# The sums of gated products for the down-projection, moved into the up-projection

## The chip, the cores and the metric

The kernel runs on one core of a Trainium2 chip. A core has a matrix engine (TensorE, PE in the profile, with PEld for its weight loads), VectorE (DVE), ScalarE (ACT) and GpSimd (POOL), each with its own instruction queue, and SyncE (SP), which here only issues DMA transfers. POOL issues transfers too. Instructions of one queue run in order; between queues, semaphores hold an instruction until what it needs is there. The metric is the device time of one execution in microseconds (us); lower is better. Before the change it is 1100.41 us, the median of three runs (1100.34, 1100.41 and 1101.11).

## The reference

A trunk of two layers over a residual of 512 tokens x 1024 features in float32. Each layer has attention (dilated sliding windows in layer 0, forgetting attention in layer 1) and then a gated feed-forward with a causal convolution, which is where the change lies:

```python
D_MODEL, SEQ, D_FF, CONV_W = 1024, 512, 2816, 3

def conv_ffn(xn, w_up, cw, cb, w_down):
    a = xn @ w_up                                    # 512 x 1024 times 1024 x 5632
    T = a.shape[1]
    ap = jnp.pad(a, ((0, 0), (CONV_W - 1, 0), (0, 0)))
    a = sum(ap[:, j:j + T] * cw[j] for j in range(CONV_W)) + cb
    gate, val = jnp.split(a, 2, axis=-1)
    return (jax.nn.gelu(gate, approximate=True) * val) @ w_down
```

## The kernel before

**Products in three parts.** A float32 operand is split into a high part, a rounded copy, and a low part, the rest. A product is then three matmuls (L289, L290 and L291, in `mm3`). A high part is a copy on ACT (`Pair.high`, L713). A low part is a subtraction on DVE (`Pair.low`, L720), or for some tiles a negated copy on ACT (L715) and an accumulating transfer that POOL issues (L716).

**The up-projection** (`ffn`). The 2816 gate columns and as many value columns are cut into 22 chunks of 128. A chunk of gate or value is a PSUM bank of 128 columns x 512 tokens. Chunks 0 and 1 come from a step ahead of the loop and chunks 20 and 21 are made plainly behind it. The 18 between are made as 9 pairs of chunks (`Pair`), in a loop over `pairs`. A pair's product is cut into 2 x 2 blocks (gate and value, halves of the inputs, halves of the tokens LO and HI) and made with seven block products p_1 to p_7 instead of eight. For that it needs sums of weight blocks (S1, S2, S3, S4; L697, on DVE), copies of partial results out of PSUM (`keep`, L736, on ACT, to tiles `csum`) and sums of results (`sum_3` L773, `sum_4` L778, `sum_1` L783, on DVE). `p_2` writes to banks that `sum_4` reads.

**Taps, gate and product.** In the iteration that makes pair i, the two chunks of pair i-1 are finished: `tap` for gate and value (ACT scales into `bb` at L635, DVE adds two shifted columns at L636 and L637), GELU on ACT (L655), and the product of both on DVE (L662) to a tile `hc` of 128 x 512. The even chunk of a pair is called a in the loop, the odd one b. When the next chunk's product is made, POOL first stores the previous `hc` to the DRAM tile hD (L660).

**The down-projection** (`down`) goes over 11 pairs j of chunks 2j and 2j+1, with the same scheme of seven products. `pair_load` reads the even chunk and the second token half of the odd one from hD into a tile `dact` (L804, L805). `pair_sums` forms three sums of 128 x 256 in it on DVE (L811 to L813), and POOL stores the last of them to the DRAM tile sD (L814). `pair_highs` and `pair_lows` split the four blocks (ACT L821, DVE L825). Later, `load_two` reads sD and the odd chunk again (L831, L832) and `pair_two` forms the remaining operands. The first pair's sums are made at the end of the up-projection's loop, those of pairs 1 to 3 during chunks 20 and 21, and the others three pairs ahead of their products.

**What sets the order.** It is written by hand: each queue has its instructions in the order in which the Python code issues them, as in this stretch of the loop's iteration (n is the next pair, p this one):

```python
            p.sum_4()
            if n and prev:
                n.high("S3")
            if prev:
                b.gelu()
            ...
            if prev:
                p.p_2()
            if n:
                n.s2()
            if prev:
                b.product()
            if n:
                n.take("A12")
                n.s4()
                n.keep_1()
```

`n.low("S3")` and `n.low("S2")` come behind it, and `prev.sum_1()`, `a.tap(0)` at the start of the next iteration. Tiles come from pools of fixed size that are reused in turn (`t8` 16 slots, `t4` 10, `t2` 8; `hc`, `csum` and the down stage's sums are from `t2`); a tile's first writer waits until the slot's last user is done. Weights arrive through `W`, which loads some blocks ahead.

Of the kernel before, what the change touches and what calls it, by code (L numbers as in the profile page):

```python
# [9 lines left out]
F32 = mybir.dt.float32  # L10
# [3 lines left out]
ALU = mybir.AluOpType  # L14

D = 1024
T = 512
# [4 lines left out]
NF = DFF // 128  # L22
# [6 lines left out]
ND = NF // 2  # L29
# [86 lines left out]
def trunk_kernel(ctx, tc, x, norm_gains, w_qkv_a, w_o_a, w_q_b, w_o_b, kv_norm, w_kvf, b_f,  # L116
                 w_up, conv_w, conv_b, w_down, rope, out):
    nc = tc.nc
    act, dve, pool, pe, sp = nc.scalar, nc.vector, nc.gpsimd, nc.tensor, nc.sync
# [8 lines left out]
    def t8(shape, dt=F32, name="t8"):  # L128
        return p8.tile(shape, dt, tag="t8", name=name)

    def t4(shape, dt=F32, name="t4"):
        return p4.tile(shape, dt, tag="t4", name=name)

    def t2(shape, dt=F32, name="t2"):
        return p2.tile(shape, dt, tag="t2", name=name)
# [490 lines left out]


    def ffn(l, bd, cp, nxt, gain, ahead):
        hD = tc.dram_tile([NF, 128, T], F32, name="hD")
        sD = tc.dram_tile([ND, 128, 256], F32, name="sD")  # L630
        hc = {}

        def tap(bb, c, s, ps):
            ch = c + s * NF
# [4 lines left out]
        class Chunk:  # L639
# [15 lines left out]
                act.activation(self.bb[:, 0, :], self.bb[:, 0, :], AF.Gelu_apprx_tanh)  # L655

            def product(self):
                c = self.c
                if c - 1 in hc:
                    pool.dma_start(hD[c - 1], hc.pop(c - 1))  # L660
                hc[c] = t2([128, T], name="hc")
                dve.tensor_tensor(hc[c], self.bb[:, 0, :], self.bb[:, 1, :], ALU.mult)  # L662
                del self.bb

        xT = None
        XA, XB = [], []
# [19 lines left out]
        class Pair:  # L686
# [52 lines left out]
            def p_1(self):  # L739
                self.G = self.new_banks()  # L740
                self.prod("A11", self.at(self.G, HI), X(0), LO, True)
# [53 lines left out]

        acts, one, two, raws, later2 = {}, {}, {}, {}, {}
        H = slice(0, 512), slice(512, 1024)
        a11, s1_, s3_, s2_ = (slice(i * 256, i * 256 + 256) for i in range(4))

        def pair_load(j):  # L800

            if j < ND:
                acts[j] = k = t8([128, 1024], name="dact")
                sp.dma_start(k[:, 0:512], hD[2 * j])  # L804
                sp.dma_start(k[:, s2_], hD[2 * j + 1, :, 256:512])  # L805

        def pair_sums(j):

            pair_load(j + 1)
            k = acts[j]  # L810
            dve.tensor_tensor(k[:, s3_], k[:, a11], k[:, s1_], ALU.subtract)  # L811
            dve.tensor_tensor(k[:, s1_], k[:, s1_], k[:, s2_], ALU.add)
            dve.tensor_tensor(k[:, s2_], k[:, s1_], k[:, a11], ALU.subtract)  # L813
            pool.dma_start(sD[j], k[:, s2_])  # L814

        def pair_highs(j):

            raws[j] = [*W.take(2), acts.pop(j)]
            one[j] = [t8([128, 2, 1024], F32R, name="w") for _ in range(3)]
            for w, r in zip(one[j], raws[j]):  # L820
                act.copy(w[:, 0], r)  # L821

        def pair_lows(j):
            for w, r in zip(one[j], raws.pop(j)):
                dve.tensor_tensor(w[:, 1], r, w[:, 0].bitcast(F32), ALU.subtract)  # L825

        def load_two(j):

            if j < ND:
                later2[j] = k, r4 = t4([128, 768], name="dact2"), t2([128, 512], name="dt4")  # L830
                sp.dma_start(k[:, 0:256], sD[j])  # L831
                sp.dma_start(k[:, 256:768], hD[2 * j + 1])  # L832
                sp.dma_start(r4, dT[l][j, :, 1536:2048])

        def pair_two(j):

            if j >= ND:
                return
            r1, = W.take(1)
            load_two(j + 1)  # L840
            k, r4 = later2.pop(j)
            w, ac = t8([128, 2, 1024], F32R, name="w"), t8([128, 2048], F32R, name="w")
            t4l = t2([128, 512], F32R, name="dt4l")
            act.copy(w[:, 0], r1)
            dve.tensor_tensor(k[:, 0:256], k[:, 256:512], k[:, 0:256], ALU.subtract)
            act.copy(ac[:, 1536:2048], r4)
            act.copy(ac[:, 0:768], k)
            dve.tensor_tensor(w[:, 1], r1, w[:, 0].bitcast(F32), ALU.subtract)
            dve.tensor_tensor(t4l, r4, ac[:, 1536:2048].bitcast(F32), ALU.subtract)
            dve.tensor_tensor(ac[:, 768:1536], k, ac[:, 0:768].bitcast(F32), ALU.subtract)  # L850
            av = ac[:, 0:1536].rearrange("p (s c) -> p s c", s=2)
            two[j] = (av[:, 0], av[:, 1]), (w[:, 0], w[:, 1]), (ac[:, 1536:2048], t4l)
# [30 lines left out]
        def p_21(j, bp):  # L883
            product_of(db[bp + 2, 0], two[j][0], 2, two[j][2], H[0], bp)

        def p_12(j, bp):
            product_of(db[bp, 1], two[j][0], 0, two[j][1], H[1], bp)
# [9 lines left out]
        def down(nxt, ahead):  # L897
            pair_highs(3)
            for bp in range(2):
                for j in range(2):  # L900
                    mul_one(j, bp)
            for j in range(1, ND - 2):
                if j > 1:
                    mul_one(j, 0)
                    mul_one(j, 1)
                if j + 3 < ND:
                    pair_sums(j + 3)
                    pair_lows(j + 2)
                    pair_highs(j + 3)
                elif j + 3 == ND:  # L910
                    pair_lows(j + 2)
                    load_two(0)
            pair_two(0)
            pair_two(1)
            for bp in range(2):
                for j in (ND - 2, ND - 1):
                    mul_one(j, bp)
                combine_one(bp)
                pair_two(bp + 2)
            one.clear()  # L920
            for bp in range(2):
                for j in range(2):
                    p_21(j, bp)
                    p_1(j, bp)
            pair_two(4)

            last = range(ND - LAST, ND)
            for j in range(2, ND - 2):
                for bp in range(2):
                    p_21(j, bp)  # L930
                if 2 <= j - 2 < ND - LAST - 2:
                    p_1(j - 2, 0)
                    p_1(j - 2, 1)
                    two.pop(j - 2)
                pair_two(j + 3)
            W.n_get += 3 * ND
            for i, b in enumerate(nxt.order):
                if ahead and i < 3:
                    W.split(W.n_split + 1)
                if b >= 2:  # L940
                    nxt.half(i, 0, 1, db[b, 1])
                    for j in range(ND - 2, ND):
                        p_21(j, b - 2)
                    nxt.half(i, 1, 0, db[b, 0])
                    for bp in range(2):
                        p_1(last[0] - 2 + i, bp)
                    if ahead and i == 1:
                        W.split(W.n_split + 1)
                    continue
                narrow = nxt.narrow and i == NB - 1  # L950
                for j in last:
                    p_11(j, b, slice(0, 256) if narrow else slice(0, 512))
                if narrow:
                    nxt.part(b, 0, db[b, 0][:, 0:256], 0)
                else:
                    nxt.half(i, 0, 0, db[b, 0])
                for j in last:
                    p_12(j, b)
                if not narrow:
                    nxt.half(i, 1, 1, db[b, 1])  # L960
                    continue
                nxt.part(b, 1, db[b, 1], 512)
                for j in last:
                    p_11(j, b, slice(256, 512))
                nxt.part(b, 2, db[b, 0][:, 256:512], 256)
# [135 lines left out]
        W.ahead_dma = 2  # L1101
        W.high_added()
        nxt.mix.gain = load_gain(gain, f"gain{l}3")
        pair_sums(0)
        a, b = m
        banks = [begun[1], bank([128, T], name="up")]
        up(*begun, range(4, KD))
# [7 lines left out]
        b.tap(1)  # L1115
        b.gelu()
        pair_highs(0)
        pair_sums(1)
        last = Chunk(NF - 2, banks)
        banks = prev.new_banks()  # L1120
        up(W.get(), banks[0], range(KD))
# [3 lines left out]
        last.tap(1)  # L1125
        last.gelu()
        pair_highs(1)
        pair_sums(2)
        up(W.get(), banks[1], range(KD))
        last.product()  # L1130
        last = Chunk(NF - 1, banks)
# [2 lines left out]
        last.tap(1)  # L1134
        last.gelu()
        pair_highs(2)
        pair_sums(3)
        pair_lows(2)
        last.product()
        pool.dma_start(hD[NF - 1], hc.pop(NF - 1))  # L1140

        down(nxt, ahead)
        W.ahead = 4
# [679 lines left out]
    for n in range(N + 3):  # L1823
        live = n < N
        if live:
            j, i = units[n]
# [93 lines left out]
```

## Time and profile before

| | |
|---|---|
| median of three runs | 1100.41 us |
| the profiled execution | 1101.14 us, of it 1099.4 us span; granted clock 0.999 |
| busy in the span | PE 1090.0 us (99%), DVE 903.0 (82%), ACT 752.7 (68%), POOL 216.5 (20%) |
| DMA | 255.22 MB, mean 232 GB/s |
| `hc` stores (L660) | 44 of 256 KB, median 7.6 us to landing |
| sD stores (L814) | 22 of 128 KB, median 5.5 us to landing |
| `dact` loads from hD | 44 of 256 KB (5.8 us), 22 of 128 KB (5.0 us) |
| the pair loop | `p_2` starts between 240.05 and 382.15 us in layer 0, from 820.60 us on in layer 1 |

Rows of a timeline read: start in us from the span's begin, duration in us, engine, line, operation, output<-inputs with their shapes, and how many instructions are merged (x2). A bracket gives the engine's idle time before it and which instruction ended that. Durations of matmuls contain pipelining, so that starts, not ends, tell their pace. Rows of a table by stretch give, for each engine, its busy us and its instructions, then the granted TensorE clock, the DMA engines' busy share and GB/s.

### The profile page before, as it was taken

Reading aid. Unit: us, or ns where it says so; the run is one execution under the profiler, and the core shown is the slowest. Engines: PE = TensorE matmul, PEld = TensorE weight load, DVE = VectorE, ACT = ScalarE, POOL = GpSimd, SP = SyncE. Lnnn points to the kernel's source line nnn. Section 1 sums busy time; section 2 is a strip of 40 time slices with the busy share of each in tenths; the row PEclk is TensorE's granted clock in tenths of the full one; section 3 lists DMA queues with packets and bytes.
Section 4 is the critical chain, followed back from the end, with each engine's and each line's share of the span. In section 5 each row is a group of like instructions: output and inputs, shape, how many; then the busy total and the mean of one; then the engine's idle time right before and its main releaser. Section 6 shows DMA issues by size and latency. Waiting matters only on the chain.

```text
span 1099.4 us, 19345 instructions
## 1 busy us (share of the span) xinstructions
PE 1090.0 (99%) x7049; PEld 972.6 (88%) x7049; DVE 903.0 (82%) x1477; ACT 752.7 (68%) x1264; POOL 216.5 (20%) x337
## 2 busy tenths in 40 slices
PE   9999999999999999999999999999999999999997
PEld 6988889999999988888878888889999999988886
DVE  5897788887887789997598677868987887789994
ACT  6754576888788766576562588756888787857572
POOL 2632000122122211000001545600122122211000
PEclk9999999999999999999999999999999999999999
DMA  9699855699999999793447666783699999999862
GB/s 325 187 360 407 318 176 137 144 227 253 228 233 236 234 302 322 274 341 96 134 154 265 214 159 169 215 269 110 145 228 249 233 224 243 224 301 312 316 249 77
DMA packets 152775, 255.22 MB, mean 232 GB/s; under 512 B 12448, under 2 KB 95384, under 8 KB 152680
## 3 DMA queue, kind: packets, MB, share of 16 engines
q1 hardware_dynamic: 133480, 186.61, 51.2%
q0 software_dynamic: 19200, 67.39, 27.5%
q8 instruction: 55, 0.90, 0.3%
q14 instruction: 40, 0.33, 0.1%
HBM read 166.08 MB, written 39.63 MB: 187 GB/s over the span
## 4 chain that ended last, share of the span: by engine, by line
PE 91%; DVE 3%; issue 2%; DMA 2%; ACT 1%; POOL 0%; SPq 0%; DVEq 0%; POOLq 0%; ACTq 0%
PE up L289 13%; PE up L290 12%; PE up L291 12%; PE acc L289 9%; PE acc L291 9%; PE acc L290 9%; PE qk_ps L290 2%; PE qk_ps L289 2%; PE qk_ps L291 2%; PE s_ps L1746 2%; PE v_ps L291 2%; PE v_ps L289 2%; PE v_ps L290 2%; PE o_ps L1794 2%; PE pT_ps L1779 2%
## 5 line engine op out<-in xcount | busy, mean ns | idle before, releaser
L289 PE MATMUL up<-xsh,w 128*128 128x256 f32 x576 | 163.0, 283 | 0.0
L290 PE MATMUL up<-xsl,w 128*128 128x256 f32 x576 | 163.0, 283 | 0.0
L291 PE MATMUL up<-xsh,w 128*128 128x256 f32 x576 | 163.0, 283 | 0.0
L289 PE MATMUL acc<-w 128*128 128x512 f32 (+1 forms) x311 | 120.7, 388 | 0.3 <-DVE mix L338 0.3
L291 PE MATMUL acc<-w 128*128 128x512 f32 (+1 forms) x311 | 120.6, 388 | 0.1
L713 ACT CAST w<-wraw 128x1024 fp32r<-128x1024 f32 x92 | 94.9, 1051 | 36.0 <-DVE wraw L697 36.0
L289 PEld LDWEIGHTS up<-xsh,w 128*128 128x128 f32 x576 | 110.6, 192 | 0.0
L290 PEld LDWEIGHTS up<-xsl,w 128*128 128x128 f32 x576 | 110.6, 192 | 0.0
L291 PEld LDWEIGHTS up<-xsh,w 128*128 128x128 f32 x576 | 110.6, 192 | 0.0
L290 PE MATMUL acc<-w 128*128 128x512 f32 (+1 forms) x267 | 103.3, 387 | 0.0
L716 POOL DMA_DIRECT2D w<-wraw x54 | 45.5, 842 | 285.5 <-ACT w L715 161.5
L636 DVE SCALAR_TENSOR_TENSOR bb<-up,conv,bb 128x511 f32<-128x511 f32 x80 | 59.8, 747 | 47.9 <-ACT bb L635 47.7
L635 ACT ACTIVATE bb<-up,conv 128x512 f32<-128x512 f32 x80 | 60.0, 780 | 31.4 <-DVE up L783 22.8
L289 PE MATMUL up<-xbh,w 128*128 128x256 f32 (+1 forms) x248 | 74.4, 300 | 0.0
L289 PE MATMUL up<-xch,w 128*128 128x256 f32 (+1 forms) x248 | 74.3, 300 | 0.0
L290 PE MATMUL up<-xcl,w 128*128 128x256 f32 (+1 forms) x248 | 73.6, 297 | 0.0
L290 PE MATMUL up<-xbl,w 128*128 128x256 f32 (+1 forms) x248 | 73.6, 297 | 0.0
L291 PE MATMUL up<-xbh,w 128*128 128x256 f32 (+1 forms) x248 | 73.5, 296 | 0.0
L291 PE MATMUL up<-xch,w 128*128 128x256 f32 (+1 forms) x248 | 73.5, 296 | 0.0
L291 PEld LDWEIGHTS acc<-w 128*128 128x128 f32 x311 | 58.4, 188 | 12.6 <-DVE w L825 0.9
L289 PEld LDWEIGHTS acc<-w 128*128 128x128 f32 x311 | 58.4, 188 | 12.6 <-DVE mix L338 0.7
L58 ACT CAST w<-wraw 128x1024 fp32r<-128x1024 f32 x54 | 55.6, 1052 | 16.1 <-PE v_ps L290 6.9
(309 smaller groups left out, 3283.7 us busy)
## 6 DMA issues: line engine op xcount, KB each, us to landing
wraw<-in_w_up_dram SPq DMA_DIRECT2D x88, 512.0 KB, 7.0
w<-wraw POOLq DMA_DIRECT2D x66, 512.0 KB, 7.9
dT<-dsums SPq DMA_DIRECT2D x28, 512.0 KB, 7.5
dsums<-in_w_down_dram SPq DMA_DIRECT2D x22, 512.0 KB, 7.6
dsums<-in_w_down_dram SPq DMA_DIRECT2D x44, 256.0 KB, 6.5
hD<-hc POOLq DMA_DIRECT2D x44, 256.0 KB, 7.6
wraw<-dT SPq DMA_DIRECT2D x22, 512.0 KB, 7.5
dact<-hD SPq DMA_DIRECT2D x44, 256.0 KB, 5.8
```

The lines of the kernel that those rows point to most:

```text
L58: self.nc.scalar.copy(pair[:, 0], raw)
L289: pe.matmul(o, ah, bh, start=first, stop=False, skip_group_check=shared)
L290: pe.matmul(o, ah, bl, start=False, stop=False, skip_group_check=shared)
L291: pe.matmul(o, al, bh, start=False, stop=last, skip_group_check=shared)
L635: act.activation(bb[:, s, :], ps, AF.Identity, bias=cp[:, 3, ch:ch + 1], scale=cp[:, 2, ch:ch + 1])
L636: dve.scalar_tensor_tensor(bb[:, s, 1:], ps[:, :T - 1], cp[:, 1, ch:ch + 1], bb[:, s, 1:], ALU.mult, ALU.add)
L713: act.copy(w[:, 0], self.f[key])
L716: pool.dma_start(w[:, 1], self.f[key], accum_op=ALU.add)
L1746: pe.matmul(s[hh][:, :nn], qT[j][:, m, hh, i * 128:(i + 1) * 128], k, start=m == 0, stop=m == 1)
L1779: pe.transpose(o[:, k0 + k, :], p[:, hh, k * 128:(k + 1) * 128], ident)
L1794: pe.matmul(o[64 * hh:64 * hh + 64, i * 128:(i + 1) * 128], Vt[hd // 8][:, k, (hd % 8) * 64:(hd % 8) * 64 + 64], pT[j, i, hh][:, k, :], st ...
```

## The change

In the product of an odd chunk (`Chunk.product`) the three sums for the down-projection are formed at once, in the even chunk's tile and in a new tile `hs` from `t2`. At the begin of the next product, `send` has POOL issue three stores of 256 KB (even chunk with one sum in its second half, `hs`, odd chunk) where two were issued, one behind each product. The sums go to a DRAM tile aD in blocks of 128 x 1024 a pair, hD keeps only odd chunks, and sD is gone. In the down-projection `pair_sums` is gone: `pair_load` reads aD[j] in one transfer of 512 KB, and `load_two` takes the last sum from aD. The sums that are computed are the same.

```diff
@@ in ffn
-        hD = tc.dram_tile([NF, 128, T], F32, name="hD")
-        sD = tc.dram_tile([ND, 128, 256], F32, name="sD")
-        hc = {}
+        hD = tc.dram_tile([ND, 128, T], F32, name="hD")
+        aD = tc.dram_tile([ND, 128, 1024], F32, name="aD")
+        hc, out_of = {}, []
+        a11, s1_ = (slice(i * 256, i * 256 + 256) for i in range(2))
+
+        def send():
+            for dst, src in out_of:
+                pool.dma_start(dst, src)
+            out_of.clear()
@@ Chunk.product
-                c = self.c
-                if c - 1 in hc:
-                    pool.dma_start(hD[c - 1], hc.pop(c - 1))
+                c, j = self.c, self.c // 2
+                send()
                 hc[c] = t2([128, T], name="hc")
                 dve.tensor_tensor(hc[c], self.bb[:, 0, :], self.bb[:, 1, :], ALU.mult)
                 del self.bb
+                if c % 2:
+                    even, odd, more = hc.pop(c - 1), hc.pop(c), t2([128, T], name="hs")
+                    dve.tensor_tensor(more[:, a11], even[:, a11], even[:, s1_], ALU.subtract)
+                    dve.tensor_tensor(even[:, s1_], even[:, s1_], odd[:, s1_], ALU.add)
+                    dve.tensor_tensor(more[:, s1_], even[:, s1_], even[:, a11], ALU.subtract)
+                    out_of.extend(((aD[j, :, 0:512], even), (aD[j, :, 512:1024], more), (hD[j], odd)))
@@ the down stage's loads and sums
         def pair_load(j):
             if j < ND:
-                acts[j] = k = t8([128, 1024], name="dact")
-                sp.dma_start(k[:, 0:512], hD[2 * j])
-                sp.dma_start(k[:, s2_], hD[2 * j + 1, :, 256:512])
-
-        def pair_sums(j):
-            pair_load(j + 1)
-            k = acts[j]
-            dve.tensor_tensor(k[:, s3_], k[:, a11], k[:, s1_], ALU.subtract)
-            dve.tensor_tensor(k[:, s1_], k[:, s1_], k[:, s2_], ALU.add)
-            dve.tensor_tensor(k[:, s2_], k[:, s1_], k[:, a11], ALU.subtract)
-            pool.dma_start(sD[j], k[:, s2_])
+                acts[j] = t8([128, 1024], name="dact")
+                sp.dma_start(acts[j], aD[j])
@@ load_two
-                sp.dma_start(k[:, 0:256], sD[j])
-                sp.dma_start(k[:, 256:768], hD[2 * j + 1])
+                sp.dma_start(k[:, 0:256], aD[j, :, 768:1024])
+                sp.dma_start(k[:, 256:768], hD[j])
@@ down, and likewise at the loop's end: each pair_sums(j) becomes pair_load(j + 1)
-                    pair_sums(j + 3)
+                    pair_load(j + 4)
@@ behind the last chunk
-        pool.dma_start(hD[NF - 1], hc.pop(NF - 1))
+        send()
```

How this moves instructions shows at three places. TensorE's order is the same in both. On DVE, in the steady part of the up-projection's loop, from `sum_4` (L778) to `sum_1` (L783), with the semaphores that each waits for; before:

```order
L778 TENSOR_TENSOR up<-up,csum 128x256 [waits PE_49] x2
L697 TENSOR_TENSOR wraw<-wsum,wraw 128x1024 [waits DMASW0_49]
L662 TENSOR_TENSOR hc<-bb 128x512 [waits DVE_49,Activation_49]
L697 TENSOR_TENSOR wsum<-wraw 128x1024 [waits DMAHW7_49,DMASW1_49,DVE_49]
L720 TENSOR_TENSOR w<-wraw,w 128x1024
L720 TENSOR_TENSOR w<-wraw,w 128x1024 [waits Activation_49]
L783 TENSOR_TENSOR up<-up,csum 128x256 [waits PE_49] x2
```

and now, where every line number below the edit is 5 to 11 higher:

```order
L789 TENSOR_TENSOR up<-up,csum 128x256 [waits PE_49] x2
L708 TENSOR_TENSOR wraw<-wsum,wraw 128x1024 [waits DMASW7_49,DMASW6_49]
L667 TENSOR_TENSOR hc<-bb 128x512 [waits DMASW4_49,DVE_49,Activation_49]
L671 TENSOR_TENSOR hs<-hc 128x256 [waits DMASW1_49]
L672 TENSOR_TENSOR hc<-hc 128x256 [waits DVE_49]
L673 TENSOR_TENSOR hs<-hc 128x256 [waits DVE_49]
L708 TENSOR_TENSOR wsum<-wraw 128x1024 [waits DMAHW3_49,DMASW0_49]
L731 TENSOR_TENSOR w<-wraw,w 128x1024
L731 TENSOR_TENSOR w<-wraw,w 128x1024 [waits DMASW6_49,Activation_49]
L794 TENSOR_TENSOR up<-up,csum 128x256 [waits PE_49] x2
```

Three subtractions or additions (L671 to L673) stand between the odd chunk's product and the sum S4 of the next pair, ahead of both low parts and of `sum_1`, and the first of them waits for a transfer of POOL's queue (DMASW), as the product does now. On POOL, whose instructions here are transfer issues, over one pair and a half of the loop, before:

```order
L716 DMA w<-wraw 128x1024
L716 DMA w<-wsum 128x1024
L660 DMA hD<-hc 128x512
L716 DMA w<-wraw 128x1024 x2
L660 DMA hD<-hc 128x512
```

and now:

```order
L727 DMA w<-wraw 128x1024
L727 DMA w<-wsum 128x1024
L727 DMA w<-wraw 128x1024 x2
L636 DMA aD<-hc 128x512
L636 DMA aD<-hs 128x512
L636 DMA hD<-hc 128x512
```

The store between S1's accumulating transfer and those of A11 and A12 has gone behind A12's, where three stores follow one another. On DVE at the end of the up-projection and the start of the down-projection, before (the two first pairs of rows of `pair_lows` with what is between them):

```order
L811 TENSOR_TENSOR dact<-dact 128x256
L812 TENSOR_TENSOR dact<-dact 128x256
L813 TENSOR_TENSOR dact<-dact 128x256
L825 TENSOR_TENSOR w<-wraw,w 128x1024 x2
L825 TENSOR_TENSOR w<-dact,w 128x1024
L662 TENSOR_TENSOR hc<-bb 128x512
```

and now:

```order
L825 TENSOR_TENSOR w<-wraw,w 128x1024 x2
L825 TENSOR_TENSOR w<-dact,w 128x1024
L667 TENSOR_TENSOR hc<-bb 128x512
L671 TENSOR_TENSOR hs<-hc 128x256
L672 TENSOR_TENSOR hc<-hc 128x256
L673 TENSOR_TENSOR hs<-hc 128x256
```

The three sums ahead of each pair's low parts are gone, and from there on DVE has only the low parts (L825) of pair after pair; the last chunk's sums stand behind its product.

More of the change, by code (lines that the diff above doesn't have):

```diff
@@ L797, in ffn @@
         H = slice(0, 512), slice(512, 1024)
-        a11, s1_, s3_, s2_ = (slice(i * 256, i * 256 + 256) for i in range(4))
         def pair_load(j):
             if j < ND:
-                acts[j] = k = t8([128, 1024], name="dact")
-                sp.dma_start(k[:, 0:512], hD[2 * j])
-                sp.dma_start(k[:, s2_], hD[2 * j + 1, :, 256:512])
-        def pair_sums(j):
-            pair_load(j + 1)
-            k = acts[j]
-            dve.tensor_tensor(k[:, s3_], k[:, a11], k[:, s1_], ALU.subtract)
-            dve.tensor_tensor(k[:, s1_], k[:, s1_], k[:, s2_], ALU.add)
-            dve.tensor_tensor(k[:, s2_], k[:, s1_], k[:, a11], ALU.subtract)
-            pool.dma_start(sD[j], k[:, s2_])
+                acts[j] = t8([128, 1024], name="dact")
+                sp.dma_start(acts[j], aD[j])
         def pair_highs(j):
@@ L1103, in ffn @@
         nxt.mix.gain = load_gain(gain, f"gain{l}3")
-        pair_sums(0)
+        pair_load(1)
         a, b = m
@@ L1117, in ffn @@
         pair_highs(0)
-        pair_sums(1)
+        pair_load(2)
         last = Chunk(NF - 2, banks)
@@ L1127, in ffn @@
         pair_highs(1)
-        pair_sums(2)
+        pair_load(3)
         up(W.get(), banks[1], range(KD))
@@ L1136, in ffn @@
         pair_highs(2)
-        pair_sums(3)
+        pair_load(4)
         pair_lows(2)
         last.product()
-        pool.dma_start(hD[NF - 1], hc.pop(NF - 1))
+        send()
         down(nxt, ahead)
```

## The prediction

> **What bounds the kernel now.** I read the page's head first, then busy time by stretch of the program, then the timelines of TensorE, VectorE and ScalarE over one pair of the up-projection.
>
> ```profile
> span 1099.4 us, 19345 instructions
> PE 1090.0 (99%) x7049; PEld 972.6 (88%) x7049; DVE 903.0 (82%) x1477; ACT 752.7 (68%) x1264; POOL 216.5 (20%) x337
> ```
>
> TensorE is busy for 1090.0 of 1099.4 us, so hardly any time can be won beside it; the question is whether the change makes TensorE wait. The busy time of the engines in 100 us of the pair loop and in 60 us of the down-projection (the last two figures are the DMA share and GB/s):
>
> ```profile
> 240.00:340.00 100.00, 100.00 (x829) 99.47 (x828) 84.12 (x113) 79.32 (x114) 22.45 (x30) 1.00 0.98 236
> 400.00:440.00 40.00, 39.96 (x177) 32.78 (x176) 39.41 (x52) 25.73 (x28) 5.40 (x10) 1.00 0.90 313
> 440.00:460.00 20.00, 20.00 (x90) 16.57 (x89) 18.82 (x24) 10.58 (x13) 1.08 (x2) 1.00 0.97 351
> ```
>
> In the loop VectorE (DVE) is busy for 84% and ScalarE (ACT) for 79%; in the down-projection DVE is nearly full, 39.41 of 40 us, yet TensorE stands still for no more than 0.04 us of it. Since matmul ends are modelled, a short stall shows in the starts. TensorE around the begin of p_2 in two pairs three apart, and in layer 1:
>
> ```profile
> 300.85 0.28 PE L291 MATMUL up<-xbh,w 128*128 128x256 f32 x1
> 301.05 0.39 PE L289 MATMUL up<-xbh,w 128*128 128x256 f32 x1
> ...
> 362.03 0.39 PE L289 MATMUL up<-xbh,w 128*128 128x256 f32 x1
> ...
> 881.27 0.28 PE L290 MATMUL up<-xcl,w 128*128 128x256 f32 x1
> 881.39 0.28 PE L291 MATMUL up<-xch,w 128*128 128x256 f32 x1
> 881.58 0.39 PE L289 MATMUL up<-xch,w 128*128 128x256 f32 x1
> ```
>
> These matmuls start 0.12 us apart (881.27, 881.39); into p_2 the step is 0.20 and 0.19. From 301.05 to 362.03 are three pairs, 20.33 us each, while a pair's matmuls alone are 7 products x 2 banks x 4 row blocks x 3 = 168 x 0.12 = 20.16 us. So TensorE already waits by some 0.1 to 0.2 us a pair, and only at p_2: this stage is balanced to a hair between TensorE and something else. What else is in DVE's timeline for the same pair:
>
> ```profile
> 294.14 0.75 DVE L636 SCALAR_TENSOR_TENSOR bb<-up,conv,bb 128x511 f32<-128x511 f32 x1 [0.73 <-ACT bb L635]
> ...
> 300.57 0.75 DVE L778 TENSOR_TENSOR up<-up,csum 128x256 f32<-128x256 f32 x2
> ...
> 302.37 0.68 DVE L662 TENSOR_TENSOR hc<-bb 128x512 f32<-128x512 f32 x1
> 302.97 1.22 DVE L697 TENSOR_TENSOR wsum<-wraw 128x1024 f32<-128x1024 f32 x1
> 304.11 2.35 DVE L720 TENSOR_TENSOR w<-wraw,w 128x1024 fp32r<-128x1024 f32 x2
> 306.38 0.42 DVE L783 TENSOR_TENSOR up<-up,csum 128x256 f32<-128x256 f32 x1
> ```
>
> and in ScalarE's, over the same stretch:
>
> ```profile
> 286.56 0.78 ACT L635 ACTIVATE bb<-up,conv 128x512 f32<-128x512 f32 x1 [0.79 <-DVE up L783]
> ...
> 289.14 0.36 ACT L736 COPY csum<-up 128x256 f32<-128x256 f32 x1
> 289.65 0.37 ACT L736 COPY csum<-up 128x256 f32<-128x256 f32 x1 [0.16 <-PE up L291]
> ...
> 291.54 0.38 ACT L736 COPY csum<-up 128x256 f32<-128x256 f32 x1
> 292.54 0.38 ACT L736 COPY csum<-up 128x256 f32<-128x256 f32 x1 [0.62 <-PE up L291]
> ...
> 293.34 1.44 ACT L635 ACTIVATE bb<-up,conv 128x512 f32<-128x512 f32 x2
> ...
> 306.89 0.78 ACT L635 ACTIVATE bb<-up,conv 128x512 f32<-128x512 f32 x1 [0.79 <-DVE up L783]
> ```
>
> The first of the two sum_4 (L778) starts at 300.57 and takes about 0.42; p_2 starts at 301.05, right behind it. So p_2 waits for sum_4, and sum_4 sits in DVE's order behind the tap of 294.14, which waited for ACT. Follow that round. DVE works without a break from 294.14 to sum_1 at 306.38: 12.24 us. ACT's bias step needs sum_1 and starts at 306.89: 0.51. ACT's own order takes it from a bias step (286.56) to the two bias steps at 293.34: 6.78. DVE's tap follows at 294.14: 0.80. The sum, 12.24 + 0.51 + 6.78 + 0.80 = 20.33, is the pair's period. **The loop is a ring DVE, ACT, DVE, as long as a pair, and TensorE follows it.** The only slack in the ring is ACT's two waits for TensorE, 0.16 + 0.62 = 0.78 us.
>
> **The change part by part.** Removed in the down-projection are pair_sums' three subtractions and its store; added in the up-projection are the same three, behind the odd chunk's product. What they cost is in DVE's timeline of the down stage:
>
> ```profile
> 411.69 0.42 DVE L811 TENSOR_TENSOR dact<-dact 128x256 f32<-128x256 f32 x1
> 412.14 0.42 DVE L812 TENSOR_TENSOR dact<-dact 128x256 f32<-128x256 f32 x1
> 412.60 0.43 DVE L813 TENSOR_TENSOR dact<-dact 128x256 f32<-128x256 f32 x1
> 412.94 2.35 DVE L825 TENSOR_TENSOR w<-wraw,w 128x1024 fp32r<-128x1024 f32 x2
> ```
>
> From 411.69 to 412.94 it is 1.25 us for the three. In the loop they stand between L662 (302.37) and L697 (302.97), with the S4 sum, the two low parts and sum_1 queued behind them, so *inside the ring*. ACT then starts 1.25 us later and its waits for TensorE vanish: 1.25 - 0.78 = 0.47 us stay. A wait also costs a start-up that back-to-back copies lack: with no wait the pair of copies takes 0.63 us in all, starting 0.25 us apart, as in
>
> ```profile
> 302.63 0.63 ACT L736 COPY csum<-up 128x256 f32<-128x256 f32 x2
> ```
>
> In the pair shown the copies start 289.65 - 289.14 = 0.51 and 292.54 - 291.54 = 1.00 apart, so from start to start the gain is 0.26 + 0.75 = 1.01, and 0.24 stays. I take **0.3 us a pair**, nearer the start-to-start count, which is how the ring was added up. The bounds of this term are 0 (something else of the pair gives way) and 1.25 (nothing does).
>
> The second limit behind p_2 is p_7, which needs S3's low part, the first of L720 at 304.11, done by about 305.3. From 301.05 on p_2 and p_3 are 48 matmuls x 0.12 = 5.8 us, so p_7 starts at 306.8: 1.5 us of slack, and 1.25 fits, barely. I cost it at nothing; if its cover is gone, it is worth what exceeds 1.5.
>
> Pairs at the ends. Pair 0's sums come behind chunk 1. ACT's timeline there, and in the last pair of the loop:
>
> ```profile
> 230.93 0.40 ACT L736 COPY csum<-up 128x256 f32<-128x256 f32 x1
> 231.54 0.37 ACT L736 COPY csum<-up 128x256 f32<-128x256 f32 x1 [0.22 <-PE up L291]
> ...
> 367.82 0.78 ACT L635 ACTIVATE bb<-up,conv 128x512 f32<-128x512 f32 x1 [2.63 <-DVE up L783]
> ...
> 375.47 1.48 ACT L635 ACTIVATE bb<-up,conv 128x512 f32<-128x512 f32 x2
> ```
>
> Only 0.22, or 0.61 - 0.25 = 0.36 by start to start, is to be recovered at 231.54, so 0.9 stays. In the last pair of the loop ACT runs from 367.82 to 375.47 without a wait (it has extra high parts there), so nearly all stays: 1.2. The six pairs between lose 0.3 each. The sums of pair 8 (from 382.9 on) take the place of pair_sums(0) and cost nothing.
>
> In the down-projection DVE is relieved of 1.25 us a pair. TensorE is hardly held there, so this is worth only what one gap in its starts shows:
>
> ```profile
> 409.73 0.39 PE L289 MATMUL acc<-w 128*128 128x512 f32 x1
> 409.95 0.39 PE L290 MATMUL acc<-w 128*128 128x512 f32 x1
> 410.38 0.50 PE L291 MATMUL acc<-w 128*128 128x512 f32 x1
> ```
>
> 0.43 where 0.22 is usual: -0.2 us a layer. The bounds are 0 and -0.2.
>
> Transfers. GpSimd's queue (POOL) gets three stores of 256 KB a pair in one place where it had two in two places; the store of 128 KB in the down stage goes, and its two loads become one of 512 KB on SyncE's queue (SP). Each issue takes POOL 0.85 us or so, and POOL is 22% busy, so the issues cost nothing. A load of the down stage runs one pair ahead as before, and its bytes are the same with the store's counted (512 KB for 384 + 128), so I cost it at nothing too. The bytes are the question. Ahead of the three stands A12's accumulating transfer, which p_2 needs. Its issue in POOL's timeline, its size and time to landing by the DMA view of 308 to 313 us, and the landings of all issues of this line in the loop:
>
> ```profile
> 309.86 0.84 POOL L716 DMA_DIRECT2D w<-wraw  x1 [2.61 <-ACT csum L736]
> ```
>
> ```profile
> w<-wraw POOLq DMA_DIRECT2D x1, 512.0 KB, 9.4
> ```
>
> ```profile
> DMA to landing us min/median/max: 5.1/8.0/10.8
> ```
>
> It lands at 319.3, and p_2 begins at 301.05 + 20.33 = 321.4: 2.1 us of slack. The two stores that are new at this place, 512 KB, take 2.2 us at the loop's 236 GB/s; by then p_2 is itself 0.3 later. I cost it at nothing, since no pair shows it late now; the upper bounds are 2.2 - 2.1 = 0.1 us a pair, or 1.5 where the landing is the longest of the row, 10.8. The new wait is DVE's: the tile of the difference takes a slot of the pool of eight whose store has to have landed. The stores of the pair before are issued from about 310.4 on, DVE needs the slot at 302.97 + 20.6 = 323.6, 13 us later, and landings of 9.4 us are shown. What is queued behind it is the whole ring, so each us beyond 13 would cost up to 1 us a pair; I cost it at nothing.
>
> **The sum.** A layer: 0.9 + 6 x 0.3 + 1.2 - 0.2 = 3.7 us; two layers 7.4. The profiled execution took 1101.14 us, the span and 1.7 around it; 1101.1 + 7.4 = 1108.5. The median of the three runs, 1100.41, is 0.7 below that execution, so the forecast is 1107.8, rounded to **1108 us**. With 0.24 to 0.47 a pair it is 1107 to 1110; with the ends at nothing or in full, 1105 to 1112.
>
> **The rivals.**
>
> *The transfers bound the loop.* For it speaks the DMA share of 0.98 in the loop: 256 KB more a pair are 1.11 us at 236 GB/s, and 20.33 x 0.98 + 1.11 = 21.0 us would be the pair's period instead of about 20.6. Against it: at 351 GB/s, which the row 440 to 460 shows, 256 KB take 0.75, and the pair would fit in 20.7. Price: 0.4 us x 8 pairs x 2 layers = 6.4 more, about 1114; 20%. The Trainium skill (DMA: Bandwidth & Descriptors, section "Issuing engines are not separate DMA queues") speaks for this one: transfers of all issuing engines run on the same 16 DMA engines and interleave, so that POOL's otherwise idle queue gives no capacity of its own. The trace agrees as far as one share of 0.98 counts both queues' work.
>
> *The stores land too late for their slots.* If three stores in a row take 13.5 us to land instead of 9.4, half a us of the ring's DVE part goes in each pair: 0.5 x 8 x 2 = 8 more, about 1116; 5%.
>
> *Not slower.* DVE stands idle for 100 - 84.12 = 15.9%, 3.2 us of each pair, and 1.25 fits in it more than twice. It decides if the ring's ACT part gives way by the full 1.25 instead of 0.78 to 1.0, because the bias step behind sum_1 doesn't set the next tap. Then the loop stays at 20.33 and only the down stage's -0.2 a layer is left: 1100.0. Against it: the idle time stands before the taps, where DVE waits for ACT, and the sums come behind them, where DVE has no idle time until sum_1. 14%. The Trainium skill (Perfetto Trace Analysis, section "Optimization Strategy") would have this case: where the most-contended engine changes between regimes, interleaving them may help. Here the trace shows DVE fullest in the regime that the work leaves, but the ring in the one it goes to.
>
> That the change does something else than it says is out: TensorE's order is the same, and DVE's shows the subtractions at the new place.
>
> **Chances and range.** Forecast 61% (1105 to 1112), transfers 20%, slots 5%, not slower 14%. A difference of 0.2%, 2.2 us, is about what can be told from no change. Of the 14%, 10 lie within 0.2% and 4 below it; all the rest is slower, 86%. The range is 1103 to 1116: it leaves out the not-slower case and what lies beyond the transfers' price.
>
> **What would show it.** The starts of p_2 in the loop 20.5 to 20.8 us apart instead of 20.33, sum_4 the last thing before each; ACT's waits of 0.16 and 0.62 for TensorE gone; in the down stage DVE clearly less busy and TensorE unchanged. Periods near 21 with p_2 held by A12's transfer are the transfers; a DVE wait ahead of the first subtraction is the slots; p_2 still 20.33 apart refutes the ring.

## The result and the profile after

The changed kernel takes 1107.61 us (median of four runs, 1107.44 to 1108.89) against 1100.38 (1100.15 to 1101.11): a ratio of 1.0065, 95% interval 1.0053 to 1.0078. It is slower by about 7 us; 1108 had been forecast. The profiled execution took 1107.65 us, with a span of 1105.9. Its head, the pair loop's window and the window of the down-projection:

```profile
PE 1092.3 (99%) x7049; PEld 973.3 (88%) x7049; DVE 902.9 (82%) x1477; ACT 749.1 (68%) x1264; POOL 216.7 (20%) x337
```

```profile
240.00:340.00 100.00, 98.69 (x814) 97.67 (x813) 88.18 (x126) 79.23 (x115) 24.42 (x34) 1.00 0.99 244
400.00:440.00 40.00, 40.00 (x179) 33.11 (x178) 38.76 (x43) 28.33 (x32) 3.21 (x6) 1.00 0.99 372
```

VectorE's work is the same over the whole span (902.9 us for 903.0) but there is more of it in the loop, 88.2 us of 100 for 84.1. TensorE now has visible gaps there, 1.3 us in 100. What they wait for, by the waits of TensorE from 222 to 400 us:

```profile
PE up L289 <- DVE up L789: 2.3, 8, 0.6
PE up L289 <- ACT csum L747: 0.2, 1, 0.2
```

L789 is sum_4, once in each of the eight iterations that make a p_2. The starts of p_2 in the fourth and the seventh of them (the seventh is the last inner pair) and in the eighth, the last pair of the loop:

```profile
302.93 0.39 PE L289 MATMUL up<-xbh,w 128*128 128x256 f32 x1 [0.19 <-DVE up L789]
...
364.75 0.38 PE L289 MATMUL up<-xbh,w 128*128 128x256 f32 x1 [0.19 <-DVE up L789]
...
386.05 0.38 PE L289 MATMUL up<-xbh,w 128*128 128x256 f32 x1 [0.62 <-DVE up L789]
```

From 302.93 to 364.75 are three pairs of 20.61 us, for 20.33 before; the last takes 21.30 for 20.12. The cycle that was forecast can be read from VectorE and ScalarE of one pair:

```profile
296.02 0.75 DVE L642 SCALAR_TENSOR_TENSOR bb<-up,conv,bb 128x511 f32<-128x511 f32 x1
...
304.25 0.69 DVE L667 TENSOR_TENSOR hc<-bb 128x512 f32<-128x512 f32 x1
304.85 0.42 DVE L671 TENSOR_TENSOR hs<-hc 128x256 f32<-128x256 f32 x1
305.30 0.43 DVE L672 TENSOR_TENSOR hc<-hc 128x256 f32<-128x256 f32 x1
305.76 0.43 DVE L673 TENSOR_TENSOR hs<-hc 128x256 f32<-128x256 f32 x1
306.11 1.22 DVE L708 TENSOR_TENSOR wsum<-wraw 128x1024 f32<-128x1024 f32 x1
...
309.51 0.76 DVE L794 TENSOR_TENSOR up<-up,csum 128x256 f32<-128x256 f32 x2
310.85 0.75 DVE L642 SCALAR_TENSOR_TENSOR bb<-up,conv,bb 128x511 f32<-128x511 f32 x1 [0.57 <-ACT bb L641]
...
313.95 0.75 DVE L642 SCALAR_TENSOR_TENSOR bb<-up,conv,bb 128x511 f32<-128x511 f32 x1 [1.57 <-ACT bb L641]
...
316.63 0.75 DVE L642 SCALAR_TENSOR_TENSOR bb<-up,conv,bb 128x511 f32<-128x511 f32 x1
```

```profile
310.03 0.78 ACT L641 ACTIVATE bb<-up,conv 128x512 f32<-128x512 f32 x1 [2.05 <-DVE up L794]
...
312.61 0.63 ACT L747 COPY csum<-up 128x256 f32<-128x256 f32 x2
...
314.73 0.66 ACT L747 COPY csum<-up 128x256 f32<-128x256 f32 x2
315.26 0.67 ACT L661 ACTIVATE bb<-bb 128x512 f32<-128x512 f32 x1
315.79 1.48 ACT L641 ACTIVATE bb<-up,conv 128x512 f32<-128x512 f32 x2
```

VectorE from chunk b's tap (296.02) to sum_1 (309.51) 13.49 us, 0.52 to ScalarE's bias step (310.03), ScalarE to the bias steps of chunk b (315.79) 5.76, 0.84 to the next tap (316.63): 20.61. Against before, VectorE's part is 1.25 longer (it was 12.24) and ScalarE's 1.02 shorter (it was 6.78): its copies at 312.61 and 314.73 follow without a wait.

Where the time lies follows from the starts of the same matmul in both profiles. Ahead of p_7 in the second iteration, the first place where it loses time in the loop, the changed kernel is 0.14 us behind (225.72 for 225.58); at p_2 of the first pair (241.12 for 240.05) 1.07, of the last inner pair (364.75 for 362.03) 2.72, of the last pair (386.05 for 382.15) 3.90, and 3.65 in the down-projection. Layer 1 repeats it: 3.11 at the same p_7 (809.24 for 806.13), then 4.04, 5.71, 6.89 and 6.65.

### The profile page after: what moved, and what is told of

It is laid out like the page before. It is cut to its first block, busy times and chain, and to the rows that moved or that the text cites. A ratio compares the mean times of both kernels' runs of the same rounds, so it can differ in the third digit from the quotient of the medians.

```text
span 1105.9 us, 19330 instructions
## 1 busy us (share of the span) xinstructions
PE 1092.3 (99%) x7049; PEld 973.3 (88%) x7049; DVE 902.9 (82%) x1477; ACT 749.1 (68%) x1264; POOL 216.7 (20%) x337
## 4 chain that ended last, share of the span: by engine, by line
PE 65%; DVE 22%; ACT 7%; issue 4%; DMA 2%; POOL 0%; DVEq 0%; ACTq 0%; POOLq 0%
PE acc L289 9%; PE acc L291 9%; PE acc L290 8%; DVE w L731 5%; PE up L289 3%; PE up L290 3%; PE up L291 3%; DVE wsum L708 3%; DVE wraw L708 3%; DVE bb L642 3%; PE qk_ps L290 2%; PE qk_ps L289 2%; PE qk_ps L291 2%; PE s_ps L1746 2%; DVE bb L643 2%
```

## The experiments

Runs without an interval are one execution with its profile; such a time is good to about 1 us, the spread of the kernel before (1100.19 to 1102.11 over fifteen runs on one chip), while periods read from the profile repeat to some 0.01 us. Where a ratio is given, both kernels ran on the same chip.

**The sums in VectorE's idle time.** The changed kernel with one difference of order: product() of an odd chunk only notes the sums, and sums_out() issues them later.

```diff
                 prev.sum_1()
                 a.tap(0)
+                sums_out()
                 ...
-            a.product()
+            a.product(True)
             ...
-                b.product()
+                b.product(True)
@@ behind the loop
         prev.sum_1()
         a.tap(0)
+        sums_out()
         a.tap(1)
```

> The changed kernel with its three sums moved to another place in VectorE's order: behind the first gate tap of the next iteration, where VectorE stands idle before the tap of the second chunk. Stores, loads and bytes stay as in the change, and the stores are issued at the same place. Ring theory (the sums cost because they lie between the tap of chunk b and sum_1, which is a cycle VectorE to ScalarE to VectorE): the starts of p_2 go back to 20.33 us apart, the first and the last pair lose nothing, and the down-projection keeps its 0.25 us a layer, so about 1099.9 us (1099 to 1101). Transfer theory (the third store of 256 KB a pair costs): the periods stay at 20.6 and the time near 1107.6. Work theory (VectorE simply has 1.25 us more to do in this stage): also 1107.6.

Measured: 1100.84 us (ten runs) against 1100.84 (thirteen), ratio 1.000, interval 0.999 to 1.001. The whole loss is gone with all stores and blocks of the change in place. VectorE at the new place, and below it the same tap in the kernel before:

```profile
288.16 0.75 DVE L643 SCALAR_TENSOR_TENSOR bb<-up,conv,bb 128x510 f32<-128x510 f32 x1
288.83 0.42 DVE L677 TENSOR_TENSOR hs<-hc 128x256 f32<-128x256 f32 x1
289.28 0.43 DVE L678 TENSOR_TENSOR hc<-hc 128x256 f32<-128x256 f32 x1
289.74 0.43 DVE L679 TENSOR_TENSOR hs<-hc 128x256 f32<-128x256 f32 x1
290.74 0.75 DVE L642 SCALAR_TENSOR_TENSOR bb<-up,conv,bb 128x511 f32<-128x511 f32 x1 [0.57 <-ACT bb L641]
```

```profile
290.75 0.75 DVE L636 SCALAR_TENSOR_TENSOR bb<-up,conv,bb 128x511 f32<-128x511 f32 x1 [1.83 <-ACT bb L635]
```

VectorE waited there for 1.83 us before, and waits 0.57 now. p_2 starts at 301.04 and, three pairs later, at 362.02: 20.33 us a pair. What did not come is the 0.25 us a layer of the down-projection: the matmul at 410 us still waits for VectorE,

```profile
410.49 0.50 PE L291 MATMUL acc<-w 128*128 128x512 f32 x1 [0.15 <-DVE w L832]
```

since the sums of the loop's last pair now stand behind the loop, where VectorE has only 0.2 us of idle time until the low parts. The run with both orders, further down, bears this out: there these sums stand at once, in the loop, and about 0.3 us is won at this place.

**A dose of work at the disputed place.** The kernel before, with nothing of the change, and k dummy subtractions behind the odd chunk's product in the loop (k = 2, 3 and 6).

```diff
                 b.product()
+                z, y = t2([128, T], name="hs"), hc[b.c]
+                for q in range(k):
+                    o, i = (a11, s1_) if q % 2 else (s1_, a11)
+                    dve.tensor_tensor(z[:, o], (z if q else y)[:, i], y[:, i], ALU.subtract)
```

> The kernel before, with two dummy subtractions of 128x256 (0.80 us in a chain, from the rows 0.45 + 0.35) behind the odd chunk's product in the loop; nothing else. Their result is not used. Ring theory: ScalarE's slack in the ring is 1.01 us, so the six inner pairs lose nothing (20.33 us), and only the last pair of each layer, which has no slack, loses about 0.7: 1101.8 us by its own profile near 1102.5. Theory that every us of VectorE's work costs in proportion (0.275 for 1.25): 0.18 a pair, 20.51 us.

> The kernel before, with three dummy subtractions in a chain (1.25 us) at the place where the change has its three sums; stores, loads and the down-projection as before. Ring theory: p_2 starts 20.60 us apart as in the changed kernel (slack 1.01, 0.24 to 0.28 stays), about 1.2 more in the last pair, so 2.8 a layer: about 1106. Transfer theory: nothing of the change's loss is here, 20.33 us and 1100.4.

> The kernel before, with six dummy subtractions in a chain at that place (5 x 0.45 + 0.35 = 2.6 us). Ring theory with a threshold: all beyond the slack of 0.98 to 1.01 stays, 1.6 us a pair, so p_2 starts 21.9 us apart; 6 x 1.6 + 2.6 = 12.2 a layer, about 1125. Proportional theory (0.275 for 1.25): 0.57 a pair, 20.9 us apart, about 1109.

The added time is read from the start of hc to that of the next sum, less the 0.60 us (302.37 to 302.97) that it takes in the kernel before. For k = 6, and p_2 in two pairs that are five apart:

```profile
307.76 0.68 DVE L662 TENSOR_TENSOR hc<-bb 128x512 f32<-128x512 f32 x1
308.48 0.42 DVE L1086 TENSOR_TENSOR hs<-hc 128x256 f32<-128x256 f32 x1
308.94 2.26 DVE L1086 TENSOR_TENSOR hs<-hs,hc 128x256 f32<-128x256 f32 x5
311.12 1.22 DVE L697 TENSOR_TENSOR wsum<-wraw 128x1024 f32<-128x1024 f32 x1
```

```profile
262.20 0.39 PE L289 MATMUL up<-xbh,w 128*128 128x256 f32 x1 [0.61 <-DVE up L778]
...
372.79 0.39 PE L289 MATMUL up<-xbh,w 128*128 128x256 f32 x1 [0.61 <-DVE up L778]
```

| | added to VectorE's order | p_2 to p_2 | more than 20.33 | added less 0.98 | time |
|---|---|---|---|---|---|
| two operations | 0.92 us | 20.33 us | 0.00 | -0.06 | 1102.36 us |
| the change | 1.26 | 20.61 | 0.28 | 0.28 | 1107.61 |
| three operations | 1.39 | 20.73 | 0.40 | 0.41 | 1108.09 |
| six operations | 2.76 | 22.12 | 1.79 | 1.78 | 1127.50 |

In the inner pairs the 0.92 us of two operations cost nothing, and of the larger doses all beyond 0.98 us is paid. The 0.98 is taken from the change's own row (1.26 less 0.28); the other rows test it. What two operations cost all the same lies in the last pair of each layer, which has no slack: 20.97 us for 20.12. The proportional theory falls (it gave 20.9 us for six), and the transfers are not needed for the change's loss: three operations without any store cost as much and more. My 20.60 and 21.9 for three and six were too low because the first dummy waits for hc itself (0.72 from start to start instead of 0.60), so the chains were longer than reckoned; with their measured lengths they fit the threshold to 0.01 us.

**Two cycles, not one.** Before the change, ScalarE's waits for TensorE were in the ring: so is the ring what sets 20.33? One edit moves sum_4 ahead of the tap it followed.

```diff
             p.sum_3()
             if n and prev:
                 n.s3()
+            p.sum_4()
             if prev:
                 b.tap(1)
             if n:
                 n.high("A22", True)
                 n.p_1()
             ...
-            p.sum_4()
```

> The kernel before with one edit: sum_4 stands ahead of the odd chunk's second tap (1.43 us of VectorE's work earlier) instead of behind it. Two cycles are told apart. Theory of two cycles: before the change the pair's period of 20.33 us is set by the cycle through TensorE (p_2, p_3, p_7, p_6, then ScalarE's copy, VectorE's taps up to sum_4, p_2), while the cycle of VectorE and ScalarE alone (with sum_1) would take 20.33 - 0.98 = 19.35. So this edit frees TensorE: p_2 starts 20.16 us apart, its own work, and 0.17 x 7 a layer are won: about 1098.3. Theory of one ring (VectorE and ScalarE alone set 20.33, ScalarE's waits for TensorE are not slack): no change, 1100.6.

Measured: 1098.07 us (ten runs) against 1100.95 (fifteen), ratio 0.9975, interval 0.9966 to 0.9984. p_2 (240.13) now follows its neighbour by 0.12 us, and the pair takes 20.16 us:

```profile
240.01 0.28 PE L291 MATMUL up<-xbh,w 128*128 128x256 f32 x1
240.13 0.28 PE L289 MATMUL up<-xbh,w 128*128 128x256 f32 x1
240.25 0.28 PE L290 MATMUL up<-xbl,w 128*128 128x256 f32 x1
...
361.09 0.28 PE L289 MATMUL up<-xbh,w 128*128 128x256 f32 x1
361.21 0.28 PE L290 MATMUL up<-xbl,w 128*128 128x256 f32 x1
```

(361.09 - 240.13) / 6 = 20.16. So the kernel before was held by a cycle through TensorE, with the copy keep_2, the taps and sum_4 in it, and not by VectorE and ScalarE alone. The rows of the prediction close this cycle: p_2 at 301.05 - 20.33 = 280.72, then p_2, p_3, p_7 and p_6, 96 matmuls x 0.12 = 11.52, to 292.24; the second copy of keep_2, which waited for TensorE, at 292.54; the bias steps at 293.34, the tap at 294.14, sum_4 at 300.57 and the next p_2 at 301.05. The same edit in the changed kernel:

> The same edit of sum_4 in the changed kernel. Theory of two cycles: with the sums the cycle of VectorE and ScalarE alone takes 20.6 us and this edit doesn't touch its length, so after at most a few pairs p_2 again starts 20.6 us apart; only a shift of 0.3 to 1.4 us a layer is won once: 1105 to 1107. If the cycle through TensorE still set the period, it would fall to 20.16 as without the sums: about 1102.

Measured: 1104.79 us. TensorE no longer waits for sum_4, but at p_7 for S3's low part, which stands behind the three sums and S4 in VectorE's order. The matmul of p_7 that needs it, six pairs apart, and the waits of TensorE's weight loads from 222 to 400 us:

```profile
246.49 0.38 PE L291 MATMUL up<-xsh,w 128*128 128x256 f32 x1
...
369.81 0.39 PE L291 MATMUL up<-xsh,w 128*128 128x256 f32 x1
```

```profile
PEld up L291 <- DVE w L731: 2.6, 8, 0.3
```

Six pairs, 20.55 us each: the period stays that of the ring, 0.06 us shorter. These 0.06 us lie between sum_1 and ScalarE's bias step (0.46 us for 0.52): in the changed kernel's trace a separate semaphore instruction of ScalarE stands between the two, in this one none does. Against the changed kernel 0.71 us are won in the first pair of each layer, 0.3 in the six inner pairs together and 0.06 in the last, 1.1 a layer, which is within the shift that was expected; the rest of the 2.8 us between the two times lies outside the loops.

**ScalarE's part of the ring.** If the ring is what the sums lengthen, the loss must also go when ScalarE's part is made shorter and the sums stay.

```diff
-            p.high("S4")
+            if not prev:
+                p.high("S4")
             if prev:
                 p.keep_2()
             p.p_4()
             a.gelu()
             if prev:
                 b.tap(0)
+                p.high("S4")
```

> The changed kernel, sums left where they are, with the high part of S4 (ScalarE, 0.94 us) moved behind the bias step that VectorE's tap of chunk b waits for, so out of ScalarE's part of the ring. Ring theory: the ring falls to 20.61 - 0.94 = 19.67 us, the cycle through TensorE takes over, p_2 starts 20.33 us apart in the six inner pairs, and the last pair loses 0.3 instead of 1.2; 0.9 to 1.3 a layer is left, about 1102.5. Theory that VectorE's 1.25 us of work cost by themselves, or the transfers: 20.6 us and 1107.6 as before.

Measured: 1105.67 us, and 20.51 us a pair instead of 20.33: (364.12 - 241.07) / 6. A miss. (In layer 1 one pair took 20.77, for a reason that stays open.) The last pair lost less, 0.40 us, as expected, but in the inner pairs only 0.1 us was won. VectorE's waits tell why:

```profile
310.51 0.75 DVE L642 SCALAR_TENSOR_TENSOR bb<-up,conv,bb 128x511 f32<-128x511 f32 x1 [0.58 <-ACT bb L641]
...
313.62 0.75 DVE L642 SCALAR_TENSOR_TENSOR bb<-up,conv,bb 128x511 f32<-128x511 f32 x1 [1.58 <-ACT bb L641]
...
316.20 0.74 DVE L642 SCALAR_TENSOR_TENSOR bb<-up,conv,bb 128x511 f32<-128x511 f32 x1
```

Chunk b's tap (316.20) now comes right behind VectorE's own work, but chunk a's second tap (313.62) still waits for ScalarE: sum_1, ScalarE's first bias step, two casts, keep_7 and the second bias step, VectorE's tap, S1, and on to the next sum_1. That is a second ring beside the first: from sum_1 at 309.17 to ScalarE's first bias step 0.52, to the second 3.09 (312.78), to VectorE's tap 0.84 (313.62) and to the next sum_1 16.06 (329.68), 20.51 us with the sums. To test this, keep_7 was taken out of it too:

```diff
                 p.high("A12", True)
-                p.keep_7()
                 p.p_6()
                 a.tap(1)
+                p.keep_7()
```

> The changed kernel, sums left where they are, S4's high part moved as in the run before, and in addition the copy keep_7 (0.51 us of ScalarE) moved behind chunk a's second bias step. The run before gave 20.51 us, not 20.33: VectorE no longer waited for ScalarE at chunk b's tap, but still at chunk a's second tap, 1.58 us. Theory of a second, parallel ring (sum_1, ScalarE's bias, casts, keep_7 and second bias of chunk a, VectorE's tap, S1 and on to sum_1), which takes 20.51 us with the sums: it is shortened by 0.51 to 20.0, the first ring is 19.67, so the cycle through TensorE sets 20.33 again and some 0.17 x 6 a layer are won against the run before: about 1103.6. Theory that something else (transfers, VectorE's work) holds 20.5: no change, 1105.7.

Measured: 1103.38 us, and p_2 20.33 us apart in all inner pairs:

```profile
240.43 0.38 PE L289 MATMUL up<-xbh,w 128*128 128x256 f32 x1
...
362.40 0.39 PE L289 MATMUL up<-xbh,w 128*128 128x256 f32 x1
```

(362.40 - 240.43) / 6 = 20.33. With 1.25 us of sums at the disputed place, the inner pairs lose nothing once both rings are shorter on ScalarE's side. The ends of the loop still do, and so the kernel stays 2.9 us above the kernel before. The last pair loses 1.07 us again, for 0.40 in the run before: ScalarE has more high parts there, and TensorE now waits for the copy keep_7 behind them, by the waits of its weight loads from 222 to 400 us:

```profile
PEld up L289 <- ACT csum L747: 1.0, 1, 1.0
```

That 1103.38 came so near the 1103.6 expected is therefore luck in part: against the run before, the inner pairs won 2.4 us (2.0 had been reckoned) and the first pairs 0.6, and the last pairs lost 1.3.

**Both orders together, and the transfers.** The late sums (the last pair's at once, in its idle time) with the early sum_4:

```diff
-                b.product(True)
+                b.product(bool(n))
             ...
+            p.sum_4()
             if prev:
                 b.tap(1)
             ...
-            p.sum_4()
```

> Both orders together: the change's sums behind the first gate tap of the next iteration (only the last pair's at once, where VectorE stands idle), and sum_4 ahead of the odd chunk's second tap. Theory of two cycles: neither cycle reaches TensorE's own 20.16 us, so 0.17 x 7 a layer are won, and the down-projection's 0.25 a layer stay: 1097.8 (1097 to 1098.6). If the sums need VectorE's idle time for which sum_4 was early, or the transfers cost, 1100 or more.

Measured: 1097.59 us (five runs, 1097.35 to 1097.80) against 1100.95, ratio 0.9967, interval 0.9955 to 0.9980: faster than both kernels. On this one, two more stores of 256 KB a pair to a tile that is not read:

```diff
-                    out_of.extend(((aD[j, :, 0:512], even), (aD[j, :, 512:1024], more), (hD[j], odd)))
+                    out_of.extend(((eD[j, :, 0:512], even), (eD[j, :, 512:1024], odd),
+                                   (aD[j, :, 0:512], even), (aD[j, :, 512:1024], more), (hD[j], odd)))
```

> The kernel with late sums and early sum_4 (1097.6 us, p_2 every 20.16 us), with two more stores of 256 KB a pair to a DRAM tile that nobody reads: five stores a pair instead of three, 512 KB more, where the change added 256 KB. Theory that transfers have room in the loop (the DMA share of 0.98 is no limit): the period stays at 20.16 us or within 0.1 of it, 1097.6 to 1099. Theory that they bound it: 512 KB at 252 GB/s are 2.1 us a pair, up to 22 us a pair and about 1130.

Measured: 1099.13 us. The loop's window without and with the two stores:

```profile
240.00:340.00 100.00, 100.00 (x835) 100.00 (x835) 90.89 (x130) 80.08 (x115) 25.36 (x35) 1.00 1.01 252
```

```profile
240.00:340.00 100.00, 100.00 (x836) 100.00 (x835) 90.90 (x130) 80.14 (x115) 30.59 (x45) 1.00 1.04 280
```

TensorE runs through in both, at 20.16 us a pair. The 1.5 us more come outside the pairs: by the starts of the same matmul 0.44 at 390 us, behind layer 0's loop, and about 1.4 in layer 1's attention between 600 and 700 us, less 0.3 at the very end; none of it in the loops. At 390 us it is a transfer that TensorE waits for, by the waits of its weight loads from 222 to 420 us:

```profile
PEld up L291 <- DMA w<-wraw: 0.6, 1, 0.6
```

No run without the two stores shows such a wait there, so five stores a pair seem to cost something once, where layer 0's loop ends; layer 1 shows none. What of the 1.4 us in the attention belongs to the stores is open, since that stretch differs by up to 1 us between runs whose code is the same there.

## Why the prediction was right, and where not

- *The place and its price.* The sums cost because they stand in a cycle of VectorE and ScalarE: shown, by taking them out of it (no loss), by dummy work in it (the same loss), and by shortening ScalarE's part (no loss in the inner pairs).
- *The terms, per layer.* First pair 0.9: measured 1.07 - 0.14 = 0.93 and 4.04 - 3.11 = 0.93. Inner pairs 6 x 0.3 = 1.8: 1.65 and 1.67, that is 0.28 each. Last pair 1.2: 1.18 in both. Down-projection -0.2: -0.25 and -0.24. The sum, 3.7 a layer, was 3.51 and 3.54, 7.05 in all for 7.4. Of the two counts of ScalarE's slack, the one from start to start (1.01) was right, 0.98 by the dose; the idle marks (0.78) undercounted it, for a copy that waits also starts later behind its neighbour. The medians differ by 7.23 us, the two profiled executions by 6.5, since the changed kernel's is 0.5 shorter between the two loops. That 1108 and 1107.61 agree to 0.4 us is thus luck in part; the terms themselves agree to 0.2 us a layer.
- *What failed.* "The loop is a ring DVE, ACT, DVE, as long as a pair, and TensorE follows it" was wrong for the kernel before. Four pieces that add up to the period are no proof, for one of them contained ScalarE's waits for TensorE. Without these the ring is 19.35 us long; 20.33 was set by the cycle through TensorE, as moving sum_4 showed. The sum came out right, although the cycle that set 20.33 was another, because the waits had been taken off as slack. The ring became the bound only with the sums.
- *What was missed.* A second ring, through chunk a's second tap, 0.1 us shorter than the first. It changes nothing in the forecast, but it made the expectation of 20.33 us for S4's late cast wrong.
- *The S3 cover.* "1.25 fits, barely" held in the inner pairs: in the changed kernel p_7 waited for S3's low part only in the second iteration of each layer, where it had been costed at nothing too (0.30 us of the first pair's 0.93), and it is the next to wait when sum_4 is early.
- *The rivals.* Transfers: refuted for the loop; 0.5 MB a pair more than the change's own stores leave the period as it is, so a DMA share near 1 was no limit there, though behind layer 0's loop one late transfer held TensorE for 0.6 us. The rule weighed there from the Trainium skill (DMA: Bandwidth & Descriptors, section "Issuing engines are not separate DMA queues") is not in doubt by that; in the loop the engines that all queues share had room. Slots: the first of the three sums follows hc without an idle mark, so no late store was seen. Not slower: true in its premise (VectorE's 3.2 us of idle time a pair can hold the sums, as the late sums show) and false for the place that the change chose.
- Most of the profiled kernel before's excess over its median, about 0.5 us, lies in layer 1's attention between 617 and 700 us; the changed kernel's profile and most others are shorter there by 0.4 to 0.8, two are longer. It is no part of the change.

## What to carry to other kernels

Where an engine is 84% busy, ask not whether there is room but in which gaps it lies, and whether the new work stands inside a cycle of engines that is nearly as long as the period; the same 1.25 us a pair cost 7 us in all at one place and nothing when they stood some 6 us later in the pair. Add up each cycle without the waits in it: only then its slack shows, and work up to the slack is free while all beyond it is paid in full, pair after pair. When one cycle is relieved, look for the one right behind it before forecasting the gain.

## What the runs showed of the hardware that was not expected

A DMA share of 1.04 at 280 GB/s in the loop went along with TensorE running through, so the busy share of the DMA engines as shown did not tell how much more they could move: it was 0.98 at 236 GB/s in the kernel before, 1.01 at 252 with both orders and 1.04 at 280 with the two stores more. And a chain of dependent 128x256 operations on VectorE steps by 0.45 us (304.85, 305.30, 305.76), while the sum S4, which reads nothing of them, follows the last by 0.35 (306.11). The first dummy, behind a 128x512 product that it reads, came 0.72 us after that product's start, where operations that do not read it followed at 0.60: 0.12 us, as it seems for the dependence.
